# Moving layer 1's first in-projection beside layer 0's second output stage in a two-layer hybrid trunk

## The chip, the cores and the metric

The kernel runs on one core of one Trainium2 chip. The metric is the device time in microseconds (us) of one execution. Five engines of the core matter here, each with a queue of its own that it works off in order: TensorE (PE; weight loads are listed apart as PEld), VectorE (DVE), ScalarE (ACT), GpSimd (POOL), and SyncE (SP), which in this kernel issues every DMA. Tiles that hold operands lie in SBUF, and products are accumulated in PSUM.

## The reference

Two layers (`DEPTH`) over 16 meta tokens and 1,024 tokens, width 1,024, all in float32. Each layer adds a mixer and an MLP to the residual `h`:

```python
for layer in range(DEPTH):
    hn = rmsnorm(h, norm_mix_w[layer])
    proj = hn @ w_in[layer]                        # 1024 x 3336
    y_a = hgrn2_mixer(...)                         # 4 heads, chunked recurrence
    y_b = gdn_mixer(...)                           # 4 heads, conv, triangular solve, recurrence
    y_c = s5_mixer(...)                            # diagonal state space, 16 groups
    h = h + concatenate([y_a, y_b, y_c]) @ w_out[layer]
    hn = rmsnorm(h, norm_mlp_w[layer])
    h = h + square(relu(hn @ mlp_w1[layer])) @ mlp_w2[layer]
return rmsnorm(h, final_norm_w)[:, N_META:]
```

All mixers are causal, so the second half of the sequence needs the states that the first half leaves, layer by layer.

## The kernel before

The 1,040 tokens are cut into two blocks b of T = 520. For each layer l and block b there are two stages. The **input stage** is `block` (line 715). `normed_rows` makes the normalized operand, 16 tiles of 128 x 524: eight chunks of the width, each split into a high and a low fp32r part. 26 products with `w_in` and a narrow one follow (`in_s5`, `in_rows`, `in_conv`, `in_gate`, `in_hgrn`), and between them the gated-delta-net's decay matrices (`gdn_decay`) and its triangular solve (`gdn_solve`, line 874, a chain of small DVE and POOL operations that ends with four stores, line 909). In a layer's first block the S5 tables are made too (`s5_layer`, again mostly small DVE operations). `hgrn` runs twice. Last comes the state phase (`gdn_state` for 5 windows x 2 head pairs, and `s5`). The **output stage** is `out_mlp` (line 1279): 8 products with `w_out`, then the MLP in 8 groups of 4 products `first` and 8 products `second`.

A product is a row of matmuls, 48 for an inner width of 1,024 and 24 for 512, three for each chunk and each 260-column half (high x high, low x high, high x low). It accumulates in one of two PSUM tiles `pd`, which DVE or ACT must read out before the tile serves the product after next. The weights come in granules of 256 KB: a DMA to `wr` (line 481), a cast by ACT to `wh` (line 459), a subtraction by POOL to `wl`; there are three buffers of each. All weight loads, stores and reloads stand in one SP queue.

What sets the order: the code is traced once, and a scheduler places the instructions on each engine's queue by priority, which is program order, as their inputs and tiles come free. An instruction that is written later can move up beside earlier work if its tiles are free. `run` writes the stages so: input (0,0), input (0,1), output (0,0), input (1,0), output (0,1), input (1,1), output (1,0), output (1,1), where (l,b) is layer and block. Input (1,0) needs the `h` that output (0,0) leaves; output (0,1) doesn't depend on input (1,0). But both take their operands from the tiles `xh` and `xl`, 8 buffers each (`operand`, line 500): output (0,1) puts `w_out`'s last three chunks there, so that its products start only when input (1,0) has made its last product. The state phase works in tiles of its own, `mt` (11 buffers), `qt` (2) and `D2` (3).

Of the kernel before, what the change touches and what calls it, by code (L numbers as in the profile page):

```python
# [10 lines left out]
F32R = mybir.dt.float32r  # L11
# [6 lines left out]
D = 1024  # L18
SEQ = 1024
NMETA = 16  # L20
DEPTH = 2
T = 520
# [3 lines left out]
GAP_DECAY, GAP_STATE, GAP_S5 = 2, 6, 4  # L26
# [4 lines left out]
NW = T // W  # L31
# [3 lines left out]
NB = 2  # L35
# [9 lines left out]
HIST = 4  # L45
# [39 lines left out]

def trace(*gens):

    live = list(gens)
    while live:
        for g in list(live):  # L90
            if next(g, StopIteration) is StopIteration:
                live.remove(g)


class Kern:
# [40 lines left out]
        return self.tl(self.sp, [128, T + 8], "s", N_S, dt)[:, :self.nt]  # L136

    def m(self, dt=F32):
        return self.tl(self.sp, [128, T], "m" + self.grp, N_M[self.grp], dt)

    def n(self, shape):
        t = self.tl(self.sp, [128, T // 2], "n" + self.grp, N_N[self.grp])
# [4 lines left out]
        return v.rearrange("p (a b) -> p a b", a=shape[1]) if len(shape) == 3 else v  # L147

    def big6(self):
        return self.tl(self.sp, [128, T], "q" + self.grp, N_Q[self.grp])  # L150

    def mps(self, grp=None):
        grp = grp or self.grp
# [346 lines left out]
    def operand(self, tag):  # L500
        return self.tl(self.big, [128, T + HIST], tag, 8, F32R)

    def normed_rows(self, h, wcol, b):

        nc = self.nc
        xs = [], []
        acc = self.s()
        for k in range(KD):
            self.square(acc, h[k], k)
        self.squares, self.r = acc, None  # L510
        r = self.scale()
        if b == 0:
            self.hist = self.tl(self.big, [128, KD, HIST], "hist", 1)
        for k in range(KD):
            w = self.prm[:, wcol + k:wcol + k + 1]
            xn = self.tl(self.sp, [128, T + 8], "s", N_S)[:, :T + HIST]
            if b == 0:
                nc.gpsimd.memset(xn[:, :HIST], 0.0)
            else:
                nc.gpsimd.tensor_copy(xn[:, :HIST], self.hist[:, k])  # L520
            self.stt(xn[:, HIST:], h[k], w, r, ALU.mult, ALU.mult)
            if b == 0:
                nc.gpsimd.tensor_copy(self.hist[:, k], xn[:, T:])
            hi, lo = self.operand("xh"), self.operand("xl")
            nc.scalar.copy(hi, xn)
            self.tt(lo, xn, hi.bitcast(F32), ALU.subtract)
            xs[0].append(hi)
            xs[1].append(lo)
        return xs
# [185 lines left out]
    def block(self, l, b, h, hook=None, first=False):  # L715

        xs = self.normed_rows(h, 8 * l, b)
        if first:
            self.save_h(b, h)
        self.Y = self.YS[b] = self.tl(self.dr, [KD, 128, T], "ydr", 2)  # L720
        if first:
            self.setup_mixers()
        g = {"z": self.tl(self.dr, [6, 128, T], "gated", 2)}
        us = self.in_s5(l, xs)
        g["rows"] = self.in_rows(l, b, xs)
        g["qkv"] = self.QKV = self.tl(self.dr, [12, 128, T], "qkvd", 2)
        self.gdn_begin(l, b, g)
        for p in range(2):
            for i in (2 * p, 2 * p + 1, 4 + 2 * p, 5 + 2 * p):
                self.in_conv(l, b, xs, i)  # L730
            trace(pipeline([self.gdn_decay(g, w, p) for w in range(NW)], GAP_DECAY))
        self.gdn_solve()
        self.gdn_scales()
        if b == 0:
            self.s5_layer(l)
        if hook:
            trace(hook)
        for i in range(8, 12):
            self.in_conv(l, b, xs, i)
        for i in range(4):  # L740
            self.in_gate(l, xs, C_GZ + 128 * i, g["z"][i])
        for j in range(2):
            hd = self.in_hgrn(l, xs, j)
            self.in_gate(l, xs, C_HG + 128 * j, g["z"][4 + j])
            trace(self.hgrn(l, b, j, hd, g["z"][4 + j]))
# [275 lines left out]
    def s5_chunks(self, t, src, dst):  # L1021
# [29 lines left out]
        z = self.m()  # L1051
# [20 lines left out]
        for q0 in (0, 2):  # L1072
            ps = self.mps()
            for q in range(q0, q0 + 2):
                D = self.tl(self.sp, [128, 2, 256], "D2", 3)
# [201 lines left out]
        return h  # L1277

    def out_mlp(self, l, b, h, last=False):
        nc = self.nc  # L1280
        xs = [], []
        for k in range(KD):
# [5 lines left out]
        for m in range(KD):  # L1288
            ps = self.product(self.weights(self.ins["w_out"][l][:, 128 * m:128 * m + 128]), xs)
            self.tt(self.half(h[m]), self.half(h[m]), ps, ALU.add)  # L1290
        xs = self.normed(h, 16 + 8 * l)
        NG = D_FF // 512
        hid = {}
# [28 lines left out]
        def second(g):  # L1322
            for m in range(KD):
                ps = self.product(self.weights(self.ins["mlp_w2"][l][512 * g:512 * g + 512, 128 * m:128 * m + 128]), hid[g])
                self.tt(self.half(h[m]), self.half(h[m]), ps, ALU.add)
            del hid[g]

        def halves(g):
# [10 lines left out]
            return step  # L1339
        for t in self.late([lambda j=j: hidden(0, j) for j in range(2)]):  # L1340
            second_operand(0, t)
        for j in range(2, 4):
            first(0, j)
        for g in range(NG):
            if g + 1 < NG:
                first(g + 1, 0)
            elif last:
                return halves(g)
            second(g)
            if g + 1 < NG:  # L1350
                for j in range(1, 4):
                    first(g + 1, j)

    def finish(self, b, h, steps=None):

# [72 lines left out]
    def run(self):  # L1428
        self.setup()
        self.H, self.YS = {}, {}  # L1430
        nxt = {}

        def early():

            nxt[1] = self.htiles()
            yield from self.load_x(1, nxt[1])
            self.save_h(1, nxt[1])
        h = self.htiles()
        trace(self.load_x(0, h))
        self.ready = {(0, col): self.in_weights(0, col) for col in (C_SU, C_SU + 128)}  # L1440
        self.setup_norms()
        self.block(0, 0, h, early(), True)
        self.block(0, 1, nxt[1])
        for l in range(DEPTH):
            for b in range(NB):

                self.take(512 if l + 1 == DEPTH and b == 0 else T)
                h = self.get_h(b)
                steps = self.out_mlp(l, b, h, l + 1 == DEPTH and b + 1 == NB)
                if l + 1 < DEPTH:  # L1450
                    self.save_h(b, h)
                    self.block(l + 1, b, h)
                else:
                    self.finish(b, h, steps)


_INS = ['x', 'meta', 'norm_mix_w', 'norm_mlp_w', 'w_in', 'hgrn_lb_logits', 'hgrn_norm_w', 'gdn_conv_w', 'gdn_a_log',
# [26 lines left out]
```

## Time and profile before

| | us |
|---|---|
| median of three runs | 3048.2 |
| lowest and highest | 3045.2, 3051.45 |
| profiled execution, device time | 3057.18 |
| its span, first to last instruction | 3055.4 |
| PE busy | 2826.1 (92%) |
| DVE, ACT, POOL busy | 1562.6, 1298.7, 1580.1 |

The page cuts the span in 40 slices and gives each engine's busy share in tenths, and the TensorE clock that was granted in tenths of the full 2.4 GHz; the other level is 1.2 GHz. The views by window give the same for stretches that one chooses: busy time of each engine, the mean granted clock, the share of the DMA engines. A busy PE isn't PE at its peak, since the ends of matmuls are modelled.

### The profile page before, as it was taken

The page shows a single profiled execution, that of the slowest core. Times are in us where ns is not written, and L with a number is a line of the kernel's source. Part 1 is how long each engine was busy: PE and PEld are TensorE (multiplying, and loading weights), DVE is VectorE, ACT ScalarE, POOL GpSimd, SP SyncE. Part 2 cuts the span into 40 slices and gives each one's busy share as a digit, 9 for nine tenths or more (in the row PEclk, how much of TensorE's full clock was granted, in tenths as well). Part 3 has the DMA queues.
Part 4 walks back from the last instruction along what each step waited for, and adds up shares of the span by engine and source line. Part 5 has one row for each costly group of instructions (what it writes and reads, how often), then busy time and mean ns, then how long its engine had stood idle before and what let it go on. Part 6 is the DMA issues. An engine that isn't in the chain of part 4 may idle for free.

```text
span 3055.4 us, 60525 instructions
## 1 busy us (share of the span) xinstructions
PE 2826.1 (92%) x23513; PEld 2637.9 (86%) x23513; DVE 1562.6 (51%) x2905; ACT 1298.7 (43%) x2657; POOL 1580.1 (52%) x1425
## 2 busy tenths in 40 slices
PE   7776899979999989878999998988999999999998
PEld 6775889978999989878999998986777788999998
DVE  7588664685532245787453224686554222522224
ACT  4434455534433345444444334543544333433332
POOL 4555465664644445747354444676464444444442
PEclk8898899989999999999999999999999999999999
DMA  5755555744433345555443334565443333533332
GB/s 148 193 125 160 141 154 138 213 95 125 126 96 96 91 141 142 161 142 149 130 115 96 94 91 142 144 152 152 113 125 98 100 96 95 163 91 90 93 91 80
DMA packets 641610, 381.17 MB, mean 125 GB/s; under 512 B 166239, under 2 KB 599237, under 8 KB 641325
## 3 DMA queue, kind: packets, MB, share of 16 engines
q1 hardware_dynamic: 641325, 377.31, 45.2%
q8 instruction: 186, 3.05, 0.4%
q14 instruction: 99, 0.81, 0.1%
HBM read 308.52 MB, written 70.43 MB: 124 GB/s over the span
## 4 chain that ended last, share of the span: by engine, by line
PE 45%; DVE 5%; issue 1%; DMA 1%; POOL 1%; ACT 1%; SPq 0%; DVEq 0%; POOLq 0%; ACTq 0%
PE pd L125 39%; PE mxt L125 4%; PE mxh L125 1%; DVE mh L113 1%; DVE s L116 1%; POOL wl L113 0%; DVE s L113 0%; ACT s L110 0%; DMA wr<-in_w_in_dram 0%; DVE s L121 0%; DMA nh<-rowd 0%; DVE mt L113 0%; POOL mh L113 0%; DVE ul L113 0%; DVE s L642 0%
## 5 line engine op out<-in xcount | busy, mean ns | idle before, releaser
L113 POOL TENSOR_TENSOR wl<-wr,wh 128x512 fp32r<-128x512 f32 x776 | 1025.2, 1323 | 1079.5 <-ACT wh L459 1012.3
L125 PE MATMUL pd<-xh,wh 128*128 128x260 f32 (+4 forms) x3688 | 832.3, 299 | 59.2 <-DVE s L116 21.2
L125 PE MATMUL pd<-xl,wh 128*128 128x260 f32 (+3 forms) x3688 | 830.1, 298 | 17.8 <-DVE xl L113 10.4
L459 ACT CAST wh<-wr 128x512 fp32r<-128x512 f32 x776 | 477.5, 617 | 862.5 <-PE pd L125 774.5
L125 PE MATMUL pd<-xh,wl 128*128 128x260 f32 (+2 forms) x3624 | 814.1, 299 | 11.0 <-POOL wl L113 10.7
L125 PEld LDWEIGHTS pd<-xh,wh 128*128 128x128 f32 (+1 forms) x3688 | 593.1, 192 | 81.4 <-issue 28.6
L125 PEld LDWEIGHTS pd<-xl,wh 128*128 128x128 f32 (+1 forms) x3688 | 594.4, 192 | 34.4 <-DVE xl L113 12.3
L125 PEld LDWEIGHTS pd<-xh,wl 128*128 128x128 f32 x3624 | 586.3, 193 | 27.2 <-POOL wl L113 13.5
L125 PE MATMUL pd<-uh,wh 128*128 128x260 f32 (+1 forms) x2008 | 469.5, 302 | 6.2 <-DVE h L113 3.6
L125 PE MATMUL pd<-ul,wh 128*128 128x260 f32 (+1 forms) x2008 | 470.5, 302 | 0.0
L125 PE MATMUL pd<-uh,wl 128*128 128x260 f32 (+1 forms) x2008 | 468.5, 302 | 1.2 <-POOL wl L113 1.2
L113 DVE TENSOR_TENSOR h<-h,pd 128x520 f32<-128x520 f32 (+2 forms) x296 | 200.4, 678 | 398.1 <-PE pd L125 395.5
L110 ACT ACTIVATE s<-s 128x520 f32<-128x520 f32 (+3 forms) x431 | 272.9, 635 | 196.5 <-DVE s L121 144.8
L125 PEld LDWEIGHTS pd<-uh,wh 128*128 128x128 f32 x2008 | 321.2, 189 | 22.3 <-issue 5.9
L125 PEld LDWEIGHTS pd<-uh,wl 128*128 128x128 f32 x2008 | 321.2, 189 | 15.4 <-POOL wl L113 2.1
L125 PEld LDWEIGHTS pd<-ul,wh 128*128 128x128 f32 x2008 | 321.4, 189 | 12.8
L116 DVE SCALAR_TENSOR_TENSOR s<-pd,r 128x520 f32<-128x520 f32 (+2 forms) x121 | 83.6, 692 | 330.8 <-PE pd L125 330.5
L113 DVE TENSOR_TENSOR ul<-s,uh 128x520 fp32r<-128x520 f32 (+1 forms) x129 | 97.7, 758 | 143.4 <-ACT uh L459 143.2
L113 POOL TENSOR_TENSOR s<-s 128x520 f32<-128x520 f32 x80 | 109.6, 1370 | 78.7 <-ACT s L110 67.9
L116 DVE SCALAR_TENSOR_TENSOR s<-pd,cvw,s 128x520 f32<-128x520 f32 x144 | 108.6, 754 | 46.4 <-ACT s L110 41.6
L113 POOL TENSOR_TENSOR mh<-mh,qh 128x260 f32<-128x260 f32 (+5 forms) x128 | 102.8, 827 | 29.9 <-ACT mh L110 29.3
L113 DVE TENSOR_TENSOR s<-s 128x520 f32<-128x520 f32 (+3 forms) x119 | 106.0, 895 | 21.8 <-ACT s L110 20.5
(255 smaller groups left out, 3187.9 us busy)
## 6 DMA issues: line engine op xcount, KB each, us to landing
wr<-in_mlp_w_dram SPq DMA_DIRECT2D x512, 256.0 KB
wr<-in_w_in_dram SPq DMA_DIRECT2D x208, 256.0 KB
wr<-in_w_out_dram SPq DMA_DIRECT2D x64, 256.0 KB
qkvd<-s SPq DMA_DIRECT2D x48, 260.0 KB
win<-qkvd SPq DMA_DIRECT2D x40, 312.0 KB
hdr<-h SPq DMA_DIRECT2D x32, 260.0 KB
mh<-qkvd SPq DMA_DIRECT2D x40, 208.0 KB
hd<-s SPq DMA_DIRECT2D x32, 260.0 KB
```

The lines of the kernel that those rows point to most:

```text
L110: return self.nc.scalar.activation(out, in_, func, **kw)
L113: return (eng or self.nc.vector).tensor_tensor(out, a, b, op)
L116: return self.nc.vector.scalar_tensor_tensor(out, a, s, b, op0, op1)
L125: return self.nc.tensor.matmul(out, lhsT, rhs, start=start, stop=stop, **kw)
L459: self.nc.scalar.copy(hi, src)
```

## The change

`block` is cut in three: `normed_rows`, a generator `projection` (all products, decays, solve, S5 tables and `hgrn`), and `states`. `out_mlp` becomes a generator as well. `run` finishes output (0,0), makes the operand of input (1,0) in 16 tiles of the state phase (`spare_operands`: 11 of `mt`, 2 of `qt`, 3 of `D2`, which are made 4 columns wider for it), and then writes `projection(1, 0)` and output (0,1) in turns, by a count that each generator yields. `states(1, 0)` follows, then what is left of output (0,1), then input (1,1), and the two output stages of layer 1. No instruction is added or left out: both programs have 20,674 matmuls, and on PE the same 5,575 of them between the last matmul of output (0,0) and the last of output (0,1).

```diff
     def m(self, dt=F32):
-        return self.tl(self.sp, [128, T], "m" + self.grp, N_M[self.grp], dt)
+        return self.tl(self.sp, [128, T + HIST * (self.grp == "t")], "m" + self.grp, N_M[self.grp], dt)[:, :T]
...
+    def spare_operands(self):
+
+        for tag, bufs in (("mt", N_M["t"]), ("qt", N_Q["t"]), ("D2", 3)):
+            for _ in range(bufs):
+                yield self.tl(self.sp, [128, T + HIST], tag, bufs, F32R)
...
-            hi, lo = self.operand("xh"), self.operand("xl")
+            hi, lo = (next(spare), next(spare)) if spare else (self.operand("xh"), self.operand("xl"))
...
+    def projection(self, l, b, xs, hook=None, first=False):
+
+
+        DENSE, MIX = 2, 0.5
...
         for p in range(2):
             for i in (2 * p, 2 * p + 1, 4 + 2 * p, 5 + 2 * p):
                 self.in_conv(l, b, xs, i)
-            trace(pipeline([self.gdn_decay(g, w, p) for w in range(NW)], GAP_DECAY))
+                yield DENSE
+            for _ in pipeline([self.gdn_decay(g, w, p) for w in range(NW)], GAP_DECAY):
+                yield MIX
...
-        for l in range(DEPTH):
-            for b in range(NB):
-
-                self.take(512 if l + 1 == DEPTH and b == 0 else T)
-                h = self.get_h(b)
-                steps = self.out_mlp(l, b, h, l + 1 == DEPTH and b + 1 == NB)
-                if l + 1 < DEPTH:
-                    self.save_h(b, h)
-                    self.block(l + 1, b, h)
-                else:
-                    self.finish(b, h, steps)
+        h = self.get_h(0)
+        trace(self.out_mlp(0, 0, h))
+        xs = self.normed_rows(h, 8, 0, self.spare_operands())
+        self.save_h(0, h)
+
+        h = self.get_h(1)
+        rest = self.out_mlp(0, 1, h)
+        due = 0
+        for n in self.projection(1, 0, xs):
+            due += n
+            while due > 0:
+                due -= next(rest, 1e6)
+        self.states(1, 0)
+        trace(rest)
+        self.save_h(1, h)
+        self.block(1, 1, h)
```

SP's queue early in input (1,0), before the change; `wr` are weight granules, `rowd` and `qkvd` what the projection stores and reloads:

```order
L481 DMA wr<-in_w_in_dram 128x4x128 x7
L161 DMA rowd<-s 68x520
L656 DMA qkvd<-s 128x520
L790 DMA mh<-rowd 68x520
L822 DMA nh<-rowd 104x2x104
L822 DMA nt<-rowd 128x2x104
```

The same place after the change:

```order
L481 DMA wr<-in_w_out_dram 128x4x128 x2
L481 DMA wr<-in_w_in_dram 128x4x128 x2
L481 DMA wr<-in_w_out_dram 128x4x128 x2
L481 DMA wr<-in_w_in_dram 128x4x128 x2
L481 DMA wr<-in_w_out_dram 128x4x128 x2
L161 DMA rowd<-s 68x520
L481 DMA wr<-in_w_in_dram 128x4x128
```

Granules of `w_out`, for output (0,1), now alternate with those of `w_in`, one product of each, where only `w_in` stood.

SP's queue around the four stores with which `gdn_solve` ends, before (line 909):

```order
L481 DMA wr<-in_w_in_dram 128x4x128 x2
L161 DMA hd<-s 128x520
L754 DMA qh<-hd 128x520
L909 DMA XD<-Tm 40x26x26 x2
L909 DMA XD<-diag 40x26x26 x2
L481 DMA wr<-in_w_in_dram 128x4x128 x2
```

And after (the line is now 935):

```order
L481 DMA wr<-in_mlp_w_dram 128x4x128 x2
L935 DMA XD<-Tm 40x26x26
L481 DMA wr<-in_w_in_dram 128x4x128
L935 DMA XD<-Tm 40x26x26
L481 DMA wr<-in_w_in_dram 128x4x128
L935 DMA XD<-diag 40x26x26 x2
```

The stores moved up against the products (they stand beside the third part of `in_conv` now, not beside `hgrn`'s products), but weight granules still stand right behind them.

DVE's queue in the last part of the solve, before; `s<-pd` empties a PSUM tile of a product:

```order
L113 TENSOR_TENSOR mh<-Tm,diag 80x507 x2
L113 TENSOR_TENSOR mh<-Tm,diag 80x169
L121 TENSOR_SCALAR s<-pd 128x520
L903 TENSOR_REDUCE nh<-mh 80x39 x2
L903 TENSOR_REDUCE nh<-mh 80x13
L903 TENSOR_REDUCE nh<-mh 80x39
```

And after:

```order
L116 SCALAR_TENSOR_TENSOR s<-pd,r 128x520
L113 TENSOR_TENSOR mh<-Tm,diag 80x507 x2
L113 TENSOR_TENSOR mh<-Tm,diag 80x169
L929 TENSOR_REDUCE nh<-mh 80x39 x3
L929 TENSOR_REDUCE nh<-mh 80x13
L113 TENSOR_TENSOR ul<-s,uh 128x520
L121 TENSOR_SCALAR nh<-nh 128x256
```

The solve's own row of operations is the same; what empties PSUM around it is now an output product (`s<-pd,r`, `ul<-s,uh`) as well as a projection's.

## Rows read from the trace of the kernel before

**Rows 1.** The page: busy tenths and granted clock in 40 slices of 76.4 us.

```profile
PE   7776899979999989878999998988999999999998
PEclk8898899989999999999999999999999999999999
```

**Rows 2.** Windows: start:end, length, busy us (instructions) by engine, clock, DMA share, GB/s.

```profile
1130.60:1154.20 23.60, 15.46 (x103) 14.63 (x103) 14.89 (x24) 10.02 (x19) 12.35 (x21) 0.78 0.68 188
1154.20:1276.00 121.80, 114.19 (x923) 112.55 (x922) 80.41 (x134) 68.15 (x151) 81.49 (x70) 0.97 0.61 162
1276.00:1320.00 44.00, 28.47 (x193) 26.49 (x192) 39.07 (x119) 15.45 (x27) 22.69 (x14) 0.83 0.51 87
1320.00:1340.20 20.20, 20.20 (x161) 20.20 (x160) 16.71 (x47) 9.45 (x18) 10.36 (x10) 0.94 0.74 216
1340.20:1400.00 59.80, 51.23 (x423) 48.13 (x422) 51.34 (x78) 24.96 (x51) 30.63 (x24) 1.00 0.51 147
1400.00:1440.00 40.00, 32.65 (x469) 29.49 (x469) 32.03 (x58) 16.47 (x32) 30.09 (x33) 0.90 0.49 144
1440.00:1480.00 40.00, 38.72 (x379) 35.68 (x380) 19.74 (x44) 18.58 (x46) 18.44 (x16) 0.93 0.56 136
1480.00:1644.40 164.40, 163.51 (x1647) 152.01 (x1645) 81.49 (x171) 74.16 (x180) 83.11 (x89) 1.00 0.41 110
1644.40:1886.30 241.90, 241.59 (x2007) 241.17 (x2005) 66.60 (x93) 82.79 (x135) 109.64 (x86) 1.00 0.35 104
```

**Rows 3.** Windows of layer 0, where other stages already stand beside each other.

```profile
420.00:580.00 160.00, 158.23 (x1609) 149.29 (x1608) 86.57 (x180) 94.12 (x226) 107.39 (x108) 1.00 0.62 167
636.00:680.00 44.00, 26.69 (x194) 24.98 (x193) 36.56 (x42) 18.34 (x32) 34.42 (x27) 0.82 0.42 71
680.00:910.00 230.00, 228.18 (x2470) 211.85 (x2467) 119.03 (x261) 98.14 (x237) 119.22 (x129) 1.00 0.43 117
```

**Rows 4.** PE's timeline where output (0,0) ends: start, us, what, idle before it.

```profile
1130.21 0.40 PE L125 MATMUL pd<-uh,wl 128*128 128x260 f32 x2
1133.86 1.19 PE L125 MATMUL pd<-s,ones 128*128 128x260 f32 x4 [3.26 <-DVE s L113]
1137.92 1.24 PE L125 MATMUL pd<-xh,wh 128*128 128x264 f32 x4 [2.87 <-ACT xh L525]
```

**Rows 5.** DVE's timeline at the same place.

```profile
1133.64 0.69 DVE L113 TENSOR_TENSOR ul<-ys,uh 128x520 fp32r<-128x520 f32 x1
1136.39 4.11 DVE L116 SCALAR_TENSOR_TENSOR s<-h,prm,r 128x520 f32<-128x520 f32 x6 [2.06 <-ACT r L110]
```

**Rows 6.** Waits, 1276 to 1320: who waited for whom, us, times, longest.

```profile
ACT wh L459 <- DMA wr<-in_w_in_dram: 8.8, 2, 8.0
PE pd L125 <- ACT wh L459: 7.2, 1, 7.2
...
SPq L909 <- DVE mh L113: 6.9, 1, 6.9
```

**Rows 7.** DVE's timeline in the solve's last part.

```profile
1282.77 5.38 DVE L113 TENSOR_TENSOR mh<-Tm,diag 80x507 f32<-80x507 f32 x3
1288.07 0.68 DVE L121 TENSOR_SCALAR s<-pd 128x520 f32<-128x520 f32 x1
...
1291.57 4.99 DVE L113 TENSOR_TENSOR mh<-nh,Tm 80x507 f32<-80x507 f32 x3
```

**Rows 8.** PE's waits, 1340.2 to 1440.

```profile
PE mxt L125 <- DMA D<-D: 5.4, 2, 3.0
PE mxh L433 <- DVE mh L113: 3.4, 2, 2.8
```

**Rows 9.** PE's waits in layer 0, 580 to 910.

```profile
PE pd L125 <- DVE xl L116: 7.4, 2, 4.5
```

**Rows 10.** The state phase's stores of line 1017 (ten, one an item), states (1,0), then (0,1).

```profile
L1017 SPq DMA_DIRECT2D ydr<-nt x10: 359/363/474, 1458.2 to 1645.8; - x10
...
L1017 SPq DMA_DIRECT2D ydr<-nt x10: 359/366/381, 717.9 to 914.0; - x10
```

More of the change, by code (lines that the diff above doesn't have):

```diff
@@ L149, in big6 @@
     def big6(self):
-        return self.tl(self.sp, [128, T], "q" + self.grp, N_Q[self.grp])
+        return self.tl(self.sp, [128, T + HIST * (self.grp == "t")], "q" + self.grp, N_Q[self.grp])[:, :T]
     def mps(self, grp=None):
@@ L501, in operand, with normed_rows @@
         return self.tl(self.big, [128, T + HIST], tag, 8, F32R)
-    def normed_rows(self, h, wcol, b):
+    def spare_operands(self):
+        for tag, bufs in (("mt", N_M["t"]), ("qt", N_Q["t"]), ("D2", 3)):
+            for _ in range(bufs):
+                yield self.tl(self.sp, [128, T + HIST], tag, bufs, F32R)
+    def normed_rows(self, h, wcol, b, spare=None):
         nc = self.nc
@@ L719, in block @@
             self.save_h(b, h)
+        trace(self.projection(l, b, xs, hook, first))
+        self.states(l, b)
+    def projection(self, l, b, xs, hook=None, first=False):
+        DENSE, MIX = 2, 0.5
         self.Y = self.YS[b] = self.tl(self.dr, [KD, 128, T], "ydr", 2)
@@ L724, in block @@
         us = self.in_s5(l, xs)
+        yield 2 * DENSE
         g["rows"] = self.in_rows(l, b, xs)
+        yield MIX
         g["qkv"] = self.QKV = self.tl(self.dr, [12, 128, T], "qkvd", 2)
@@ L730, in block @@
                 self.in_conv(l, b, xs, i)
-            trace(pipeline([self.gdn_decay(g, w, p) for w in range(NW)], GAP_DECAY))
+                yield DENSE
+            for _ in pipeline([self.gdn_decay(g, w, p) for w in range(NW)], GAP_DECAY):
+                yield MIX
         self.gdn_solve()
@@ L739, in block, with states @@
             self.in_conv(l, b, xs, i)
+            yield DENSE
         for i in range(4):
             self.in_gate(l, xs, C_GZ + 128 * i, g["z"][i])
+            yield DENSE
         for j in range(2):
             hd = self.in_hgrn(l, xs, j)
+            yield 3 * DENSE
             self.in_gate(l, xs, C_HG + 128 * j, g["z"][4 + j])
-            trace(self.hgrn(l, b, j, hd, g["z"][4 + j]))
+            yield DENSE
+            for _ in self.hgrn(l, b, j, hd, g["z"][4 + j]):
+                yield MIX
+        self.mixed = g, us
+    def states(self, l, b):
+        g, us = self.mixed
         self.grp = "t"
@@ L1074, in s5_chunks @@
             for q in range(q0, q0 + 2):
-                D = self.tl(self.sp, [128, 2, 256], "D2", 3)
+                D = self.tl(self.sp, [128, T + HIST], "D2", 3)[:, :512].rearrange("p (h r) -> p h r", h=2)
                 nc.sync.dma_start(D, self.D02[8 * t + 2 * q:8 * t + 2 * q + 2].rearrange("g p r -> p g r"))
@@ L1290, in out_mlp @@
             self.tt(self.half(h[m]), self.half(h[m]), ps, ALU.add)
+            yield 2
         xs = self.normed(h, 16 + 8 * l)
@@ L1325, in second @@
                 self.tt(self.half(h[m]), self.half(h[m]), ps, ALU.add)
+                yield 1
             del hid[g]
@@ L1341, in out_mlp @@
             second_operand(0, t)
+        yield 4
         for j in range(2, 4):
             first(0, j)
+            yield 2
         for g in range(NG):
@@ L1346, in out_mlp @@
                 first(g + 1, 0)
+                yield 2
             elif last:
-                return halves(g)
-            second(g)
+                self.steps = halves(g)
+                return
+            yield from second(g)
             if g + 1 < NG:
@@ L1352, in out_mlp @@
                     first(g + 1, j)
+                    yield 2
     def finish(self, b, h, steps=None):
@@ L1443, in run @@
         self.block(0, 1, nxt[1])
-        for l in range(DEPTH):
-            for b in range(NB):
-                self.take(512 if l + 1 == DEPTH and b == 0 else T)
-                h = self.get_h(b)
-                steps = self.out_mlp(l, b, h, l + 1 == DEPTH and b + 1 == NB)
-                if l + 1 < DEPTH:
-                    self.save_h(b, h)
-                    self.block(l + 1, b, h)
-                else:
-                    self.finish(b, h, steps)
+        h = self.get_h(0)
[13 more added lines that the diff above has]
+        self.block(1, 1, h)
+        for b in range(NB):
+            self.take(512 if b == 0 else T)
+            h = self.get_h(b)
+            self.steps = None
+            trace(self.out_mlp(1, b, h, b == 1))
+            self.finish(b, h, self.steps)
 _INS = ['x', 'meta', 'norm_mix_w', 'norm_mlp_w', 'w_in', 'hgrn_lb_logits', 'hgrn_norm_w', 'gdn_conv_w', 'gdn_a_log',
```

## The prediction

> **What bounds the kernel now.** I read the page first: PE is the engine that is nearly always busy, and it falls off, with its clock, where an input stage stands alone [rows 1]: the five slices from 1069 to 1451 us hold 8, 9, 8, 7 and 8, between rows of nines. Then I cut the part between the ends of output (0,0) and output (0,1), 1130.6 to 1886.3 us, in windows [rows 2]. The reader is to see three things there. From 1130.6 to 1340.2 (input (1,0), alone) and on to 1480 PE stands idle for a part of each window and its clock is below 1.00 in most. From 1480 on, with output products to fill in, it is idle for 1.2 us in 406. And in the windows where PE loses most, DVE is the busiest engine: 39.07 of 44 us and 51.34 of 59.8.
>
> The stretch is 755.7 us. The pure output products at its end cost 241.9 us for 2,007 matmuls, 0.1205 us each [rows 2]. By the order, 4,736 matmuls of products lie in the stretch, before as after: 570.7 us. What else there is, 185.0 us, is the work of the small matmuls (decays, `hgrn`, states) and the losses. I count a window's loss as length less PE busy, plus busy time by the missing share of the clock [rows 2]:
> - the head, to 1154.2: 8.1 + 3.4 = 11.5
> - 1154.2 to 1276: 7.6 + 3.4 = 11.0
> - 1276 to 1340.2: 15.5 + 4.8 + 1.2 = 21.5
> - 1340.2 to 1400: 8.6
> - 1400 to 1480: 8.7 + 6.0 = 14.7
> - the rest: 1.2
>
> That is 57.0 us outside the head. It is the most that a better mixture can give back. 116.5 us remain as the small matmuls' own PE time, which does not change.
>
> **The change, part by part.** Nothing is added or taken away; input (1,0)'s products, decays, solve, tables and `hgrn` get output (0,1)'s 3,456 matmuls (416.4 us) as company.
>
> *The head* stays. Output (0,0) must end, the norm must be made (PE idle 3.26 and 2.87 us, [rows 4]), and the order puts the two S5 products first, fed by the same 16 operand pieces. New in it: output (0,1)'s last three chunks of `w_out`'s operand are now split here, since `xh` and `xl` are free. That is three ACT casts, and three DVE subtractions at 0.69 us, two of them queued ahead of the six norm multiplications. DVE idles 2.06 us just there [rows 5], which covers two. One of the casts waits for a load and stands between the two ACT operations that make the norm's factor; if that load is late, the cover is gone. Cost between 0 and 2.1 us (three at 0.69); I take 1.
>
> *1154.2 to 1276* (S5, gates' rows, convolutions, decays; 11.0 us). A convolution asks DVE for four operations a product, an output product for one or two, and every second product is now one of the latter. The row nearest to this is input (0,1) beside states (0,0): 1.8 us idle in 160, clock 1.00 [rows 3]. At that rate 1.3 us stay. Give-back between 0 (each wait recurs, since both streams stand in one queue) and 11; I take 9.
>
> *1276 to 1340.2* (solve and first S5 tables; 21.5 us). DVE runs 5.38 and 4.99 us of `80x507` operations with PSUM readers queued between [rows 7], and the solve's four stores on SP wait 6.9 us for it with weight granules behind them, which is PE's longest stop, 7.2 us [rows 6]. Both are in the order after the change as well: the same burst, and granules behind the stores. The nearest row is 636 to 680, the same solve of block (0,1) beside output (0,0): it lost 17.3 + 4.8 = 22.1 us [rows 3]. But there the waits were for the MLP's own operand, `xl` [rows 9], which is not in the making at the new place. Bounds 0 and 21.5; I take 6, near the lower one, because DVE's burst is the cause and is not touched.
>
> *1340.2 to 1400* (8.6 us; the rest of the tables, `hgrn`'s start and output (0,1)'s start all at once, DVE 51.34 of 59.8). These come apart: the tables end beside convolutions and gates, `hgrn` comes a hundred us later. PE's 3.4 us for line 433, the tables' own matmul [rows 8], are likely to recur. Give-back 0 to 8.6; I take 5.
>
> *1400 to 1480* (14.7 us). 5.4 us of it are waits for S5's loads to `D` [rows 8], which stay, later: the `D2` tiles now hold operand until the last projection product. The clock should hold where products fill in. Give-back 0 to 14.7; I take 6.
>
> *The state phase* loses its early start: all 16 state tiles are taken until the last product of input (1,0), with 1,632 product matmuls left (196.7 us) as cover. Items came (1645.8 - 1458.2) / 9 = 20.8 us apart [rows 10], while PE hardly waited. By the order the last five intervals between items held 56 to 86 product matmuls and 11 to 80 of `hgrn`'s, and now hold 95 to 111 and none, so that an item gets about the time it had. I take 0; bounds 0 to 9 (9 items, 1 us each, from 21.8 us an item in states (0,1) against 20.8, [rows 10]).
>
> *Elsewhere*: the order of small work shifts a little before 1130 and after 1886, with the same instructions. 0, within 5 either way.
>
> Sum: 9 + 6 + 5 + 6 - 1 = **25 us less**. The profiled execution took 3057.2 us (its span 3055.4), 9 over the median of 3048.2, so 3032 for such an execution, and **3023** for the median.
>
> **The rivals.**
> *The stalls move along.* PE takes its matmuls in the order written, and so do DVE, ACT and SP: a stopped product of one stream stops the other. For it: the stop for the solve beside output products in layer 0, 22.1 us [rows 3]. Against it: 420 to 580 and 680 to 910, two other pairs side by side, with 1.8 us idle each [rows 3]. Then 5 us come back, of the clock: 3043. The Trainium skill bears on it ("TensorE: Matmul & The Clock Gate", "Architectural detail"): ACT and DVE queues are strictly first in, first out, and only weight loads are pulled ahead on PE. The stop of [rows 6], which runs from DVE over SP and ACT to PE, agrees.
>
> *Everything but the hard stops goes.* 57.0 less about 12 (5.4 for `D`, 6.9 for the stores) is 45 back: 3003. For it: those same two quiet windows. Against it: DVE's burst.
>
> *Slower: weights for both streams stand behind the projection's stores.* SP holds every granule, and a store that waits for a slow chain holds those behind it; now output products starve with it, where before they came after. One such stop cost 7.2 us [rows 6]. From four more on (25 / 7.2) the gain is gone; six more cost 43 and give 3048 - 25 + 43 = 3066. For it: some thirty stores and reloads of the projection among twice as many granules. Against it: twice as many products between two stores, and DMA engines that were never busier than 0.74 of a window [rows 2].
>
> That the change does not do what it says is excluded by the order.
>
> **How the numbers follow.** Forecast 0.60, its own range 3008 to 3040 (give-back 8 to 40: about half of the way to the bounds on either side, since five of them don't all err together). Stalls move along 0.17; all goes 0.14; slower 0.09. The range leaves out the slower case and half of the one at 3003: 3002 to 3046. About 0.2% (6 us) is what a measurement can tell from no change. Faster: 0.58 of the forecast, all 0.14, and 0.06 of the stalls that move along: 0.78. Same: 0.02 + 0.10 + 0.01 = 0.13. Slower 0.09.
>
> **What would show it.** Between the ends of the two output stages some 731 us instead of 755.7. Right: no window with PE under 90% except the head and the solve, whose DVE row stays near full; PE's longest wait still for a granule held by the solve's stores, or for a PSUM reader; `D` waits of about 5 us, later; items 18 to 21 us apart. Wrong: a head over 26 us; new SP waits at the projection's stores with `wr` behind them; items over 22 us apart; or a changed time before 1130.6 or after the second output stage of layer 0 that outweighs the stretch.

## The result and the profile after

Before 3048.9 us (six runs, 3045.2 to 3051.5), after 3071.1 us (six runs, 3061.3 to 3078.3): ratio 1.007, 95% interval 1.0052 to 1.0089. The change costs 22 us; 25 us less were forecast. The profiled executions took 3057.2 and 3072.9 us; of these 15.7 us the traces tell where they are. I cut each span at the last product of output (0,0) and of output (0,1):

| us | before | after | difference |
|---|---|---|---|
| start to the end of output (0,0) | 1130.6 | 1145.0 | +14.4 |
| from there to the end of output (0,1), the stretch | 755.7 | 764.6 | +8.9 |
| from there to the end of the span | 1169.1 | 1161.5 | -7.6 |

The parts of a span come from one execution of each kernel. Both traces hold 23,513 PE instructions, and 6,289 of them lie between the two cuts in both; the counts of 20,674 and 5,575 given with the change stand in no trace, but what they were given for, that both programs have the same, holds.

The two cuts in the view of PE's timeline (start, duration, engine and line, operation, in brackets the idle time before and what ended it); each is the row ahead of a norm's `ones` product. Before the change the first is in [rows 4], and the second is

```profile
1885.90 0.40 PE L125 MATMUL pd<-uh,wl 128*128 128x260 f32 x2
```

After the change:

```profile
1144.62 0.40 PE L125 MATMUL pd<-uh,wl 128*128 128x260 f32 x2
1148.27 1.21 PE L125 MATMUL pd<-s,ones 128*128 128x260 f32 x4 [3.26 <-DVE s L113]
1154.65 1.23 PE L125 MATMUL pd<-mt,wh 128*128 128x264 f32 x4 [5.17 <-ACT mt L531]
...
1909.18 0.40 PE L125 MATMUL pd<-uh,wl 128*128 128x260 f32 x2
1912.81 1.17 PE L125 MATMUL pd<-s,ones 128*128 128x260 f32 x4 [3.23 <-DVE s L113]
```

The page's slices of 76.8 us, which answer to [rows 1]:

```profile
PE   7777999979999998987999998988999999999998
...
PEclk8897899989999999998998999998999999999999
```

The five slices that held 8, 9, 8, 7, 8 from 1069 us on now hold 9, 8, 9, 8, 7, from 1075 us on: the dip is one slice further on and no shallower. The clock has new 8s in the slices from 1382, 1612 and 2073 us. The windows of the stretch, which answer to [rows 2] (window, its length, busy time and count for PE, PEld, DVE, ACT, POOL, granted clock, DMA share, GB/s):

```profile
1145.00:1167.00 22.00, 10.94 (x63) 10.09 (x63) 16.25 (x25) 10.45 (x18) 12.01 (x18) 0.69 0.61 182
...
1200.00:1240.00 40.00, 35.71 (x284) 35.32 (x283) 18.59 (x28) 16.24 (x36) 19.48 (x15) 0.96 0.40 113
1240.00:1280.00 40.00, 36.05 (x288) 35.35 (x287) 29.70 (x44) 23.60 (x54) 23.64 (x20) 0.96 0.48 129
...
1350.00:1380.00 30.00, 23.14 (x170) 22.75 (x169) 27.27 (x44) 9.35 (x16) 15.53 (x11) 0.91 0.29 78
1380.00:1412.00 32.00, 23.70 (x173) 23.12 (x173) 31.62 (x112) 12.89 (x22) 14.61 (x11) 0.82 0.55 107
1412.00:1440.00 28.00, 21.34 (x156) 20.99 (x155) 21.89 (x49) 8.61 (x15) 12.27 (x11) 0.82 0.42 111
1440.00:1480.00 40.00, 37.55 (x323) 35.86 (x322) 25.76 (x36) 15.90 (x32) 21.28 (x17) 1.00 0.63 173
...
1640.00:1680.00 40.00, 34.17 (x433) 31.81 (x431) 27.25 (x55) 14.46 (x28) 33.29 (x37) 0.89 0.41 119
1680.00:1720.00 40.00, 40.00 (x414) 37.44 (x414) 19.32 (x41) 13.32 (x37) 13.36 (x15) 0.81 0.50 124
```

By the prediction's own count (idle time of PE, and busy time by the missing share of the clock) the stretch lost 68.5 us before and 80.1 now. Input (1,0) has company now, and PE loses as much: 14.5 us in the head; 11.1 from 1200 to 1280, where 11.0 were lost alone; 32.0 from 1350 to 1440, at the solve and the S5 tables, where 30.1 were lost alone; 17.2 from 1640 to 1720, where the windows from 1480 on lost 1.2 in all before. PE's waits from 1350 to 1440 (what waited for what, us in all, times, longest):

```profile
PE mxh L417 <- DVE nh L121: 8.7, 2, 6.3
PE pd L125 <- DVE h L113: 6.4, 1, 6.4
PE pd L125 <- DVE s L116: 4.4, 1, 4.4
```

All three are DVE's queue, but not one burst of it:

```profile
1366.70 7.06 DVE L113 TENSOR_TENSOR mh<-Tm,diag 80x507 f32<-80x507 f32 x3
...
1377.19 7.36 DVE L113 TENSOR_TENSOR mh<-nh,Tm 80x507 f32<-80x507 f32 x3
...
1388.14 0.28 DVE L121 TENSOR_SCALAR nh<-nh 128x256 f32<-128x256 f32 x1
...
1419.05 0.69 DVE L113 TENSOR_TENSOR h<-h,pd 128x520 f32<-128x520 f32 x1
```

The operand of the tables' transposes (`nh`, for L417) stands behind the solve's `80x507` operations. The PSUM reader `s` (4.4 us) stands at 1363.66, behind the solve's shorter operations. The reader `h` (6.4 us) comes long after the solve, behind the tables' small operations. In [rows 6] PE's longest stop was a granule held behind the solve's stores; that one is gone, and these came in its place.

The longest wait in the new stop, at 1675, is one chain over four engines. SP, POOL, ACT and PE in that order:

```profile
1672.23 0.33 SPq L950 DMA_DIRECT2D mt<-MAd  x1
...
1674.03 0.52 SPq L848 DMA_DIRECT2D nt<-rowd  x1
...
1666.92 5.29 POOL L113 TENSOR_TENSOR mt<-mt 64x256 f32<-64x256 f32 x4 [2.60 <-DVE mt L113]
...
1678.52 0.38 ACT L110 ACTIVATE nt<-nt 128x208 f32<-128x208 f32 x1 [6.85 <-DMA nt<-rowd]
1678.80 0.36 ACT L1107 COPY mt<-mxt 128x260 f32<-128x260 f32 x1
...
1679.21 1.97 PE L125 MATMUL mxt<-mt,D 128*128 128x65 f32 x8 [3.21 <-ACT mt L1107]
```

SP issued the load of `MAd` into an `mt` tile as POOL ended a run of four operations on `mt` (1672.21), the load of `nt` stood behind it in the queue, ACT waited 6.85 us for that with the copy of PE's operand behind it. The state phase starts here beside `hgrn`'s last chains and the MLP. Of the 17.2 us lost, 5.8 are idle time and 11.4 the lower clock, 0.89 and then 0.81. That two `pd` tiles are too few to go on with over such a stop is likely, but no run tried more.

And ahead of the change, in input (0,1), the windows that answer to [rows 3]:

```profile
420.00:500.00 80.00, 75.54 (x889) 70.61 (x888) 47.17 (x86) 46.72 (x110) 59.93 (x61) 0.98 0.52 142
...
636.00:680.00 44.00, 23.77 (x164) 22.15 (x165) 30.50 (x41) 15.83 (x28) 28.58 (x25) 0.73 0.44 77
680.00:720.00 40.00, 38.56 (x540) 35.97 (x538) 27.17 (x63) 12.08 (x28) 25.91 (x32) 0.83 0.51 135
...
800.00:820.00 20.00, 15.42 (x149) 14.61 (x148) 13.85 (x20) 6.67 (x15) 15.95 (x18) 0.83 0.42 109
```

Lost: 26.6 us from 636 to 680 (22.1 before), 8.0 from 680 to 720 and 7.2 from 800 to 820, where 680 to 910 lost 1.8 before. The instructions here are the same; what differs is the width of the state phase's tiles, and with it the order in which the scheduler put them.

### The profile page after: what moved, and what is told of

Read it like the earlier page. It is cut to its first block, busy times and chain, and to the rows that moved or that the text cites. A ratio compares the mean times of both kernels' runs of the same rounds, so it can differ in the third digit from the quotient of the medians.

```text
span 3071.1 us, 60499 instructions
## 1 busy us (share of the span) xinstructions
PE 2844.3 (93%) x23513; PEld 2658.8 (87%) x23513; DVE 1571.5 (51%) x2905; ACT 1302.2 (42%) x2657; POOL 1581.0 (51%) x1425
## 4 chain that ended last, share of the span: by engine, by line
PE 68%; DVE 13%; DMA 5%; issue 2%; ACT 2%; POOL 1%; SPq 0%; DVEq 0%; POOLq 0%; ACTq 0%
PE pd L125 57%; PE mxt L125 7%; DVE mh L113 4%; PE mxh L125 2%; DVE s L116 2%; DVE s L113 1%; DMA nt<-rowd 1%; ACT s L110 1%; DMA ys<-ydr 1%; DVE s L648 1%; DVE mt L113 0%; DVE nh L113 0%; DMA nh<-rowd 0%; DVE s L121 0%; DVE h L113 0%
## 5 line engine op out<-in xcount | busy, mean ns | idle before, releaser
L125 PE MATMUL pd<-xh,wh 128*128 128x260 f32 (+3 forms) x3256 | 744.0, 301 | 47.6 <-DVE s L116 12.9
L125 PE MATMUL pd<-xl,wh 128*128 128x260 f32 (+3 forms) x3256 | 741.7, 300 | 6.8 <-DVE xl L113 4.7
L125 PE MATMUL pd<-xh,wl 128*128 128x260 f32 (+2 forms) x3208 | 729.7, 300 | 4.3 <-POOL wl L113 4.1
L125 PEld LDWEIGHTS pd<-xh,wh 128*128 128x128 f32 x3256 | 526.2, 192 | 67.3 <-issue 25.1
L125 PEld LDWEIGHTS pd<-xl,wh 128*128 128x128 f32 x3256 | 528.3, 193 | 22.7 <-DVE xl L113 5.8
L125 PEld LDWEIGHTS pd<-xh,wl 128*128 128x128 f32 x3208 | 520.5, 193 | 20.3 <-POOL wl L113 5.8
L125 PE MATMUL pd<-mt,wh 128*128 128x264 f32 (+3 forms) x594 | 106.0, 299 | 20.0 <-DVE s L116 7.7
L113 DVE TENSOR_TENSOR s<-s 128x520 f32<-128x520 f32 (+3 forms) x119 | 106.8, 902 | 26.6 <-ACT s L110 24.1
```

The costliest lines, as they stand in the source:

```text
L113: return (eng or self.nc.vector).tensor_tensor(out, a, b, op)
L125: return self.nc.tensor.matmul(out, lhsT, rhs, start=start, stop=stop, **kw)
```

## The experiments

Each kernel was timed against the kernel before on the same chip; the ratio is the measure. "Lost" is the prediction's count, summed over windows of 25 us of the stretch. Times in the expectations are in the terms of the first comparison, where the kernel before took 3048.9 us; on the other chips it took 3051.0 to 3053.6, so that only ratios are compared.

| kernel | ratio, 95% interval | output (0,0) ends | stretch | lost in it |
|---|---|---|---|---|
| before | 1 | 1130.6 | 755.7 | 68.3 |
| after | 1.0070 (1.0052, 1.0089) | 1145.0 | 764.6 | 78.9 |
| e1 wider tiles alone | 1.0053 (1.0035, 1.0072) | 1144.9 | 753.9 | 66.8 |
| e2 after, no turns | 1.0038 (1.0026, 1.0050) | 1144.7 | 753.1 | 67.9 |
| e3 turns from the solve on | 1.0048 (1.0031, 1.0064) | 1143.8 | 757.9 | 65.8 |
| e4 turns up to the solve | 1.0047 (1.0029, 1.0064) | 1144.1 | 760.4 | 75.5 |
| e5 after, tiles 520 wide | 1.0009 (0.9995, 1.0023) | 1126.2 | 757.4 | 72.6 |
| e6 e5, no turns | 0.9997 (0.9986, 1.0008) | 1125.9 | 754.5 | 68.3 |
| e7 e5, solve on DVE alone | 1.0018 (1.0005, 1.0031) | 1126.9 | 761.5 | 75.4 |
| e8 e5, turns inside the solve | 1.0014 (1.0003, 1.0025) | 1125.9 | 763.1 | 76.7 |
| e9 only `qt`, `D2` wider | 0.9999 (0.9988, 1.0010) | 1125.8 | 755.1 | 69.2 |
| e10 e5, tables in output (0,0) | 1.0005 (0.9993, 1.0018) | 1141.9 | 741.1 | 62.0 |
| e11 e6, tables in output (0,0) | 1.0012 (1.0002, 1.0021) | 1144.6 | 742.2 | 60.5 |
| e12 e10, turns from the solve on | 1.0009 (0.9999, 1.0020) | 1140.2 | 742.6 | 60.3 |
| e13 e5, solve left out | 0.9975 (0.9964, 0.9985) | 1126.7 | 747.8 | 60.0 |
| e14 e6, solve left out | 0.9969 (0.9959, 0.9979) | 1126.3 | 747.2 | 60.5 |

**The four columns.** e1 is the kernel before with

```diff
-        return self.tl(self.sp, [128, T], "m" + self.grp, N_M[self.grp], dt)
+        return self.tl(self.sp, [128, T + HIST * (self.grp == "t")], "m" + self.grp, N_M[self.grp], dt)[:, :T]
```

and the like for `qt` and `D2` (`D2` from 512 columns); e9 widens only these two.

> The kernel before, with nothing of the change but the four extra columns in the tiles mt, qt and D2. Its order on every engine is the changed kernel's, row for row, up to the end of output (0,0) and again from input (1,1) on; in between the old sequence stands. Theory 'order': the 14 us by which output (0,0) ends later in the changed kernel (1145 against 1130.6 us), and the 7 us that come back after 1909, are the scheduler's answer to the wider tiles and have nothing to do with the two streams. Then this kernel ends output (0,0) at 1145 +-3 and takes 3055 +-4. Rival 'streams': the loss belongs to the interleaving, the 14 us were that execution's chance: 3049 +-3, output (0,0) at 1131.

> The kernel before with only qt and D2 made wider (to 524 columns, five tiles) and mt left at 520. SBUF addresses behind them move, and the order of every engine is that of the kernel before, row for row. Theory 'order': no change, ratio 0.998 to 1.002, output (0,0) ends at 1126 to 1131. Rival 'layout' (other addresses and strides are what costs, not the order): output (0,0) later by some 14 x 5/16 = 4 us or more, ratio 1.0015 or above.

e1 carries most of the loss, 1.0053 of 1.0070, without a product moved: 16 us where 6 were expected. Its trace has what was expected of the parts: output (0,0) ends at 1144.9, and what follows the stretch takes 1162.1 us, 7 less than before. The 6 came out too small because the trace of the kernel before is of a long execution, 3057.2 us against a median of 3048.9: output (0,0) ends at 1130.6 in it, but between 1125.8 and 1126.9 in the seven later kernels with the same order there. e9 is level with the kernel before, so it takes the wider `mt` to bring the loss (`mt` alone was not run).

The traces bear the order out. Up to 60 us before the end of output (0,0), the kernel before, e9 and e5 below have the same operations in the same order on PE, ACT, POOL and SP; so have e1 and the changed kernel; and these two orders part at 324 us. That the wider tile itself is not slower stands in e1's trace: two groups of operations on `mt` (count, then least, median and longest ns), before, then e1:

```profile
L113 DVE TENSOR_TENSOR mt<-mxt,gsc x40: 671/680/692, 299.2 to 2353.2; 104x512 f32<-104x512 f32 x40
...
L110 ACT ACTIVATE mt<-mt x60: 618/638/643, 356.8 to 2197.9; 128x520 f32<-128x520 f32 x60
```

```profile
L113 DVE TENSOR_TENSOR mt<-mxt,gsc x40: 668/678/692, 298.4 to 2363.7; 104x512 f32<-104x512 f32 x40
...
L110 ACT ACTIVATE mt<-mt x60: 622/638/642, 353.5 to 2210.1; 128x520 f32<-128x520 f32 x60
```

So it is the order. What that does is best seen at the solve of input (0,1), in DVE's timeline. In e9, which has the old order:

```profile
641.34 0.74 DVE L116 SCALAR_TENSOR_TENSOR xl<-h,prm,xh 128x520 fp32r<-128x520 f32 x1
642.00 0.68 DVE L113 TENSOR_TENSOR h<-h,pd 128x520 f32<-128x520 f32 x1
642.61 4.26 DVE L116 SCALAR_TENSOR_TENSOR xl<-h,prm,xh 128x520 fp32r<-128x520 f32 x1
646.80 4.72 DVE L113 TENSOR_TENSOR mh<-nh,Tm 80x507 f32<-80x507 f32 x3
```

and in the changed kernel:

```profile
641.45 9.02 DVE L113 TENSOR_TENSOR mh<-nh,Tm 80x507 f32<-80x507 f32 x3
...
652.16 0.74 DVE L116 SCALAR_TENSOR_TENSOR xl<-h,prm,xh 128x520 fp32r<-128x520 f32 x1
...
653.07 0.68 DVE L113 TENSOR_TENSOR h<-h,pd 128x520 f32<-128x520 f32 x1
```

Two operands of the MLP (`xl`) and a PSUM reader (`h<-h,pd`) stood ahead of the second burst; now they stand behind it. The burst itself ends no later, at 650.5 us against 651.5: in e9 one `xl` took 4.26 us beside POOL and the three multiplications 4.72, in the changed kernel these three took 9.02. But the reader comes at 653.07 instead of 642.00. PE waits for that reader (7.2 us) and twice for ACT, from 600 to 820:

```profile
PE pd L125 <- DVE h L113: 11.8, 2, 7.2
PE mxh L125 <- ACT ph L459: 7.5, 2, 6.2
PE mxt L125 <- ACT nt L988: 6.0, 2, 4.6
```

where it waited 7.4 us for `xl` before [rows 9].

e5 is the counterproof: the whole change, turns and all, with `mt`, `qt` and `D2` left at 520. Input (1,0) opens the sequence, so the four columns ahead of it are zeros, and a convolution can have them from a memset:

```diff
-                yield self.tl(self.sp, [128, T + HIST], tag, bufs, F32R)
+                yield self.tl(self.sp, [128, T], tag, bufs, F32R)
...
+            ps = self.cols(l, C_GQ + 128 * i, xs, {0: slice(0, HN), 1: slice(HN - HIST, T)}, {0: HIST})
+            nc.vector.memset(ps[:, 0, :HIST], 0.0)
```

> The changed kernel with the tile mt left 520 wide. The operands of input (1,0) are 520 wide too; the four columns of zeros ahead of the block are written into PSUM by a DVE memset for each of the 12 convolutions (12 short instructions more, 4 columns less in 24 x 12 matmuls). Its order up to the end of output (0,0) is that of the kernel before, row for row. Theory 'order': output (0,0) ends at 1131 +-2, the stretch stays at 764 +-5, and the time is 8 us over the kernel before: ratio 1.0026 (1.001 to 1.004). Rival 'streams': the ratio stays at 1.006 or above.

Output (0,0) ends at 1126.2, and the loss falls from 1.0070 to 1.0009, with an interval that holds 1. The ratio, the end of output (0,0) and the stretch are all better than expected (1.0026, 1131 and 764), since the expectation was worked out from the two traces of the comparison. The five kernels with 524 columns end that stage between 1143.8 and 1145.0, the eight with the old order between 1125.8 and 1130.6; the means are 1144.5 and 1126.8.

**The turns.** e2, e3 and e4 keep the wide tiles; e6 is e5 without turns:

```diff
-        for n in self.projection(1, 0, xs):
-            due += n
-            while due > 0:
-                due -= next(rest, 1e6)
+        trace(self.projection(1, 0, xs))
         self.states(1, 0)
```

e3 leaves out the `yield`s ahead of `gdn_solve`, e4 those behind it.

> The changed kernel with the operands in the state phase's tiles, but with projection(1,0), states(1,0) and output (0,1) written one behind the other, not in turns. Theory 'stalls move along': the turns give nothing back and cost the new stop where hgrn, the state phase and output products meet (17 us at 1640 to 1720). Then this kernel's stretch is 755 to 765 us and its time 3055 to 3065, at or below the changed kernel's 3071. Rival 'operand tiles': the state phase's late start is what costs, and the turns do give back: then this kernel is slower than the changed one, over 3078.

> The changed kernel with output (0,1)'s products in turn only with the products behind the solve (four convolutions, the gates, hgrn); up to the solve the projection stands alone. Before the change the part ahead of the solve lost 11.0 us alone, and with company it lost 11.1. Theory 'stalls move along': company ahead of the solve is worth nothing, so this kernel stands within 5 us of the changed one, 3066 to 3076; more output products are then left for the state phase, so that its stop at 1640 to 1720 may shrink, to 3058 at the lowest. Rival 'mixture works': 9 us lost ahead of the solve, 3080.

> The complement: output (0,1)'s products in turn with the projection only up to the solve, and the projection alone from there to its end, with the rest of the output stage beside the state phase. Theory 'stalls move along': the stops behind the solve (32 us from 1350 to 1440) are the DVE burst's and stay, and the state phase has more output products left than in the changed kernel: 3060 to 3071. Rival 'mixture works': behind the solve the company gave back 8 to 10 us (1400 to 1480 before: 14.7 lost, after: 4): 3080.

> e5 without the turns: projection(1,0), states(1,0), output (0,1) written one behind the other, operands in 520-wide tiles of the state phase. Theory 'order and stalls': with the old order up to 1130 and no turns nothing is left of the loss: ratio 0.998 to 1.001, some 8 us under e5. Rival 'operand tiles cost': above 1.002, as e5.

e2, e3 and e4 fell in the range of their theory (their ratios make 3060.5, 3063.5 and 3063.2 us of 3048.9; e3 by the lower end of its range), and e6 too, though it is 4 us under e5 and not 8, with intervals that overlap. Without turns the stretch takes 753.1 to 755.7 us (before, e1, e2, e6, e9), with them 757.4 to 764.6 (after, e3, e4, e5, e7, e8). The two groups stand apart, but each figure is from one execution, and between two single kernels a few us show nothing. Over the whole stretch company gives nothing back in any of them. e3 has no stop in the state phase, as expected, and by the count it loses as little as the kernels without turns, yet its stretch is 4 us longer than e1's; the count doesn't say where. The losses of e4, e5 and the full turns are 4 to 11 us larger. The intervals of e1 to e4 overlap, so that among these only the stretches of the traces speak.

**The burst.** Does another mixture at the solve help?

```diff
-                        a[:, i0:i0 + k, :].unsqueeze(2).to_broadcast([80, k, H, H]), ALU.mult, eng=nc.gpsimd if n % 2 else None)
+                        a[:, i0:i0 + k, :].unsqueeze(2).to_broadcast([80, k, H, H]), ALU.mult, eng=nc.gpsimd if n % 2 and not dve else None)
```

is e7; e8 has `yield` behind each third row and each block of the solve, and `yield MIX` for each in `projection`.

> e5, and input (1,0)'s solve makes all ten of its 80x507 products on DVE, where POOL made four beside it. In the trace of the changed kernel one of these takes DVE 1.06 to 5.1 us while POOL makes its own, so that the six on DVE took 12.4 us there with reductions between; ten at 1.06 are 10.6. Theory 'DVE's burst stops PE, whatever the company': the stop at the solve shortens by 2 to 8 us, and the time with it: ratio 0.001 to 0.003 under e5. Rival 'the chain of the solve and the loads behind its stores stop PE': as e5 or, since POOL no longer helps, up to 5 us slower.

> e5, but the solve itself is a generator with 14 turns, so that seven products of output (0,1) are written inside it, where the changed kernel wrote the solve as one piece between two projection products. Each asks DVE for one or two operations, where a convolution asks for four. Theory 'DVE's burst stops PE, whatever the company': PE's stops between the start of the solve and the end of the S5 tables stay at 25 to 32 us; ratio within 0.0015 of e5. Rival 'the wrong company': 10 us or more come back, ratio 0.003 under e5.

The expected gain of e7 did not come, and the time is what its rival allowed: DVE's passes took 7.41 and 6.25 us for five operations each, against 5.76 and 6.13 us for the three that are DVE's in e5, and the stretch is 4 us longer. (In the changed kernel the six took 7.06 and 7.36 us, 14.4 and not 12.4.) The burst was to be shortened and was not, so that e7 doesn't decide between its theory and its rival:

```profile
1346.92 7.41 DVE L113 TENSOR_TENSOR mh<-Tm,diag 80x507 f32<-80x507 f32 x5
...
1357.77 6.25 DVE L113 TENSOR_TENSOR mh<-nh,Tm 80x507 f32<-80x507 f32 x5
```

e8 gained nothing either, as its theory had it. With output products inside the solve PE waits 18.6 us for two of DVE's PSUM readers from 1310 to 1420 (in e5 11.0 us for the same two, and 7.3 for the tables' transposes):

```profile
PE pd L125 <- DVE s L116: 9.9, 2, 5.1
PE pd L125 <- DVE h L113: 8.7, 3, 4.1
```

**Away with the causes.** e10 to e12 make layer 1's S5 tables while output (0,0) runs, where DVE has time:

```diff
-        trace(self.out_mlp(0, 0, h))
+        for n, _ in enumerate(self.out_mlp(0, 0, h)):
+            if n == 50:
+                self.s5_layer(1)
```

> e5 (520-wide operands, both streams in turns) with layer 1's S5 tables (s5_layer, some 180 small DVE operations and 8 transposes) made in the middle of output (0,0), where DVE is busy for a quarter of the time, and not behind the solve of input (1,0). Theory 'stops have causes, and the tables are one': in e5's trace PE stops 6.8 + 1.8 us for the tables' transposes and 6.5 and 2.9 us for PSUM readers queued behind the tables' operations; 10 to 18 us of these go: ratio 0.995 to 0.998. Rival 'stalls move along': the sum of the losses in the stretch, 65 to 79 us in every order so far, stays, and the time stays within 0.1% of e5.

> e6 (520-wide operands, no turns) with layer 1's S5 tables in the middle of output (0,0). It tells whether the turns are worth anything once the tables are gone from the stretch. Theory 'stops have causes': before the change the tables cost PE 8 us between 1340 and 1400 and part of the 21 us at the solve; 8 to 15 us go, ratio 0.995 to 0.998, level with e10. Rival 'the turns pay once the tables are out of the way': this one stays at 0.999 to 1.000, and e10 is 5 us or more faster.

> e10 with turns only from the solve on, as in e3. In e3 the stretch lost 66 us, the least of the kernels in turns, since the state phase was left with more output products and had no stop. Expected: at or below e10 by up to 7 us (the state phase's stop). Rival: as e10.

The stretch did shorten, by 16, 12 and 15 us against e5, e6 and e5, and the time did not: e10 and e11 missed their 0.995 to 0.998, and e12 is not under e10. Output (0,0) ends 14 to 19 us later than in e5 and e6. The tables' own PE work went along (of e10's 16 us, 10.6 are smaller losses), and they stop PE there as well. e10's window:

```profile
900.00:950.00 50.00, 43.91 (x343) 42.54 (x343) 45.63 (x144) 16.98 (x35) 21.83 (x18) 0.97 0.35 98
```

7.4 us are lost among pure MLP products, where e5 loses nothing, and DVE is busy for 45.63 of 50 with 144 instructions, where e5 has 21: the tables stand in one heap, not spread over the stage.

e13 and e14 leave out the arithmetic of input (1,0)'s solve, in turns and without:

```diff
-        for i in range(1, H):
+        for i in range(1, 1 if skip else H):
...
-        for dst, a, bt in ((mid, low(Dg), Tm[:, 0:H, 0:H]), (low(Tm), Tm[:, H:, H:], mid)):
+        for dst, a, bt in () if skip else ((mid, low(Dg), Tm[:, 0:H, 0:H]), (low(Tm), Tm[:, H:, H:], mid)):
```

> e5 with the arithmetic of input (1,0)'s solve left out (the 22 multiplications and 22 reductions on DVE and POOL; its loads, its copy on ACT and its four stores stay). It takes away the burst that the prediction held to be the cause of the stop. Theory 'the burst is the cause, with company or without': 8 to 15 us of the 25 to 30 us that PE loses from the solve to the end of the tables go, the tables' own stop (6.6 us) stays: ratio 0.996 to 0.999, stretch 742 to 750 us. Rival 'losses move along, whatever one takes away': stretch over 753 us.

> e6 (no turns) with the same arithmetic left out. If the company were worth anything at the solve, the solve would cost more here than in turns, and this kernel would gain more than e13 does against e5. Theory 'company is worth nothing there': both gain the same to 4 us. Rival 'company hides part of the solve': this one gains 6 us or more beyond e13's gain.

Both came out in the range of their theory, except that e13's stop for the tables' transposes shrank too (7.3 us in e5, 2.7 here). The solve is worth 9.6 us of the stretch with company (757.4 to 747.8) and 7.3 without (754.5 to 747.2), the same within what single executions tell. So nothing shows that output products hide any of it. Without it both lose the same, 60.0 and 60.5 us. PE's waits for DVE from 1310 to 1420 fall from 21.0 us in e5 to 13.2 in e13, and in neither does PE wait for a granule there, which speaks for DVE's queue and against the loads behind the solve's stores, e7's rival.

No kernel here that does the whole work beats the one before: e6 and e9 are level with it.

## Why the prediction was wrong

Two steps failed. The give-back failed by more: the stretch was forecast at 731 us and took 764.6. The other, *Elsewhere*, made a loss of what would have been no change: with the old order kept, the same turns give the ratio 1.0009 (e5).

*Elsewhere: 0, within 5* failed first in time. The order of small work ahead of 1130 was seen to shift and was priced at nothing, because the instructions were the same. It cost 14.4 us in this pair of executions and 17.7 by the means of the five kernels with the wide tiles and the eight with the old order; e1 has it without the streams, and e5 has the streams without it. The part behind 1886 gave 7.6 back in this pair; over all, from the end of output (0,1) to the last matmul, the five kernels are 4 us shorter than the eight (means 1154.2 and 1158.7). Together that is some 13 us, within e1's interval of 11 to 22. A stage that loses 163 us to waits and the lower clock, as the part before 1130 does by the same count, can't be given a bound of 5 when its order changes.

*The give-back, 26 us in four terms,* is the second: company was to fill PE's stops, and in sum filled none. Term by term:
- 1154 to 1276, 9 expected: 0 (11.0 before, 11.1 after). The nearest row, input (0,1) beside states (0,0) [rows 3], doesn't say what input beside an output stage does: there the state phase leaves the two `pd` tiles alone, while an output product takes its turn at them, and its reader stands in the same DVE queue (this is argued; the runs show only that nothing came back).
- Solve and tables, 6 + 5 expected: 2 us more were lost. I had the row that told it, the same solve beside output (0,0) with 22.1 us lost [rows 3], and argued it away because the waits there were for `xl` [rows 9]. The cause named, DVE's burst, was right as far as it went (without the solve's arithmetic 9.6 and 7.3 us go, e13 and e14); with another operand in the queue it stops another reader. The tables' small operations are a second such burst: PE's longest single wait here, 6.4 us for `h`, is behind them.
- 1400 to 1480, 6 expected: 10.6 (4.1 us lost from 1440 to 1560). Here products did fill in, at the better half of the bounds.
- The state phase, 0 with 9 at worst: 17.2 us. The items came 20.4 us apart, as forecast (the row below, which answers to [rows 10]); the loss is the stop at the phase's start, 5.8 us of idle time, and 11.4 of the clock, which fell to 0.81 behind it. I had costed the pace of the phase, not its beginning.

```profile
L1043 SPq DMA_DIRECT2D ydr<-nt x10: 359/366/533, 1706.6 to 1890.1; - x10
```

- The head, 1 with 2.1 at worst: 3.0. PE waits 5.17 us for ACT's first operand piece where it had waited 2.87 [rows 4].

Of the rivals, *stalls move along* had the mechanism; I gave it 0.17 and priced it 5 us faster, because I let the clock's losses come back. They stayed too: with the stops from 1350 to 1440 the clock stood at 0.91, 0.82 and 0.82, and at 0.89 and 0.81 with the one at 1675. The slower rival, granules held behind stores, did not happen; in the whole stretch PE waits 0.5 us for a granule. *What would show it* did name the case: "a changed time before 1130.6 ... that outweighs the stretch"; in the traces it came, and the stretch missed its 731 us as well.

## What to carry to other kernels

A shared scheduler makes every edit global: a tile four columns wider cost 14 us or more in stages that the change was not meant to touch. Compare the order of the untouched stages first, and where it differs, price the difference by the losses of that stage, or keep the tile's shape. Look also at where the profiled execution stands among the times: the expectations that were worked out from the long one before (3057.2 us against 3048.9) missed. And in these kernels company did not fill stops that sit in the queue of a shared reader: before two streams are put side by side, ask through which engine and which PSUM tiles both must pass, and what long burst stands in that queue.

## What the runs showed of the hardware

A DVE operation that reads two operands from SBUF took several times as long while POOL worked on SBUF. In e9 the second `xl` took 4.26 us, where the one before it took 0.74. It ended at 646.9, after the third of these POOL operations (two in the first row):

```profile
641.49 3.58 POOL L113 TENSOR_TENSOR mh<-nh,Tm 80x507 f32<-80x507 f32 x2 [2.64 <-DVE nh L903]
645.04 1.27 POOL L113 TENSOR_TENSOR mh<-qh 128x520 f32<-128x520 f32 x1
646.28 3.64 POOL L113 TENSOR_TENSOR wl<-wr,wh 128x512 fp32r<-128x512 f32 x2
```

In the changed kernel the first of the three multiplications stands in that place, and POOL's row is the same:

```profile
640.99 3.51 POOL L113 TENSOR_TENSOR mh<-nh,Tm 80x507 f32<-80x507 f32 x2 [2.19 <-DVE nh L929]
644.47 1.27 POOL L113 TENSOR_TENSOR mh<-qh 128x520 f32<-128x520 f32 x1
645.71 3.16 POOL L113 TENSOR_TENSOR wl<-wr,wh 128x512 fp32r<-128x512 f32 x2
```

So three multiplications took 4.72 us in one order and 9.02 in the other. Between, `h<-h,pd`, with one operand in PSUM, took 0.68 us in e9 while POOL worked. In e7, with POOL at work for only a part of the time, five multiplications took 6.25 us. The Trainium skill ("SBUF — State Buffer", section "SBUF: two separate sides") states that a DVE operation with two SBUF inputs and a POOL operation that reads SBUF shut each other out for a whole instruction. These rows agree; here DVE was shut out for three POOL operations on end. An operation's time from one order is therefore not its time in another.
